# A hybrid trunk layer on one core: more gate tiles as products of x without its norm, a second norm in steps, and no GpSimd arithmetic at the end

## The chip, the core and the metric

The kernel runs on one core of a Trainium2 chip. TensorE (PE) multiplies, VectorE (DVE), ScalarE (ACT) and GpSimd (POOL) work on tiles of 128 partitions, and SyncE, ACT and GpSimd issue DMAs. The time is the device time of one execution in microseconds (us), as the median of several runs. One execution is recorded by the hardware profiler; all rows below are from it.

## What is computed

One layer on 1024 tokens with 1024 features, all in float32:

```python
h = rmsnorm(x, ln1_g)
b_a, c_a, x_a, x_b, g_b, gate_a_logit, gate_b_logit = split(h @ w_in)   # 7 x 1024 columns
y_a = b_a * causal_depthwise_conv(c_a * x_a, conv_a_w)
u_b = causal_depthwise_conv(x_b, conv_b_w, conv_b_b)
y_b = rg_lru(u_b, ...) * gelu(g_b)
merged = (sigmoid(gate_a_logit + bias_a) * (y_a @ w_out_a)
          + sigmoid(gate_b_logit + bias_b) * (y_b @ w_out_b))
x = x + merged @ w_o
h = rmsnorm(x, ln2_g)
x = x + (silu(h @ w_gate) * (h @ w_up)) @ w_down      # 2816 wide
return rmsnorm(x, final_g)

def rmsnorm(x, g):
    return x * rsqrt(mean(x * x) + 1e-6) * g
```

rg_lru is a gated linear recurrence; its decay holds softplus(-lambda).

## The kernel before

**Layout.** Data lie transposed: 128 features on the partitions, 1024 tokens along the row, in two halves H0 and H1 of 512. A tensor of 1024 features is eight such tiles. A matmul takes a 128x128 block of weights and a 128x512 half.

**Precision.** Every operand is split into a high part (ACT, line 114) and the rest (DVE, line 115), and a product is three matmuls (`mm`, line 123): low by high, high by low, high by high. So each tile that PE reads costs ACT and DVE one operation each.

**Products.** Two output tiles of 128 features and the two halves of the tokens form a 2x2 scheme that is worked out with seven products, named P1 to P7, instead of eight (class `Pair`). They need sums of weight blocks (`left_form`, line 240, additions on line 251; the tiles are named s, their splits ws, splits of plain weights wa) and sums of data tiles (`form_steps`, line 149, lines 158 to 175; seven groups, named b11, t1, t2, b21, t3, t4 and b22 in the order they are made). With K = 1024 a product is 12 matmuls, and a pair 84. Results lie in PSUM banks of four tags (a, b, c and x, two banks each) and are combined by `evacuate` (line 282; operations on lines 290 to 318). The products of neighbouring pairs are interleaved: P4 and P3 of a pair come after P5 and P6 of the next.

**Order.** The program emits one product after the other, some of the weight sums of later ones, and after each product at most one step from a queue of background work (`bg`, `tick`). A scheduler puts this into one fixed order for each engine; each engine runs its own list in that order and waits on semaphores. So an operation that waits holds up all behind it on its engine.

**Stages.** (1) The start. x is read, and while the sum of squares of the norm is still running, PE multiplies x without its norm by the weights of four tiles of gate A in ordinary products (line 123 into banks a, b and c for three of them, then into x for the fourth, 48 matmuls): the norm's root R is a factor for each token and can be applied to the result (`std_out`, line 577). R comes from a sum over partitions by matmuls with ones and from `rstd` (line 134: Ln and Exp on ACT, each with a table load, then a Newton step on DVE, lines 141 to 146). Then DVE scales x by R (line 574) and the first forms are made from it. `softplus` (lines 352 to 367) is some 24 small operations for the decay. (2) 26 pairs of the input projection: 20 for the mixers, then gate A (2 pairs) and gate B (4). (3) Mixer stages and the output projections, and the residual x2 with its squares, summed in S2. (4) `norm2` (line 707): root of S2 in two halves, at once, after product P6 of the second pair of the feed-forward stage. 11 times a pair of gate and a pair of up tiles; `ev_fg` (line 717) multiplies by the root, takes Silu and multiplies again (line 715, half tiles), `ev_fu` (line 726) multiplies the two and stores them. (5) The down projection in three groups over its 2304 first rows; the last four tiles of 128 are ordinary products in three pieces of 512, 256 and 256 tokens (`Piece`, line 791), which run with the final norm: each product is added to x2 (line 804), squared on ACT (line 807), the squares of m = 1 to 5 are added on GpSimd (line 809), sums of the rest go through PE (bank x), and `step` (line 825) scales the result: on DVE (line 834), or, for the m in the piece's list `pool`, by ACT (line 813) and GpSimd (line 832).

Of the kernel before, what the change touches and what calls it, by code (L numbers as in the profile page):

```python
# [13 lines left out]
P = 128  # L14
# [13 lines left out]
PIECES = ((0, 512, (1, 4)), (512, 256, (1, 4, 6)), (768, 256, (1, 4, 6)))  # L28
# [21 lines left out]
def trunk(ctx: ExitStack, tc: tile.TileContext, xT, w_first, w_std, w_in, w_ob, w_oa, w_o, w_gu, wd0, wd1, wd2, w_dl,  # L50
# [485 lines left out]

    def first_mm(k):
        for n in range(3):
            std_mm(k, wfs[k], slice(n * P, (n + 1) * P), std[n])
# [3 lines left out]
    R = wide("R")  # L543
    for k in range(KT):
# [11 lines left out]
        if k == 0:  # L556
            nc.scalar.activation(S, x, AF.Square)
        else:
            sq = wide("sq")
            nc.scalar.activation(sq, x, AF.Square)  # L560
            nc.vector.tensor_add(S, S, sq)
        if k == KT - 1:
            sum_split(S, sums, lambda s: wide(s, F32R)[:, :HN])
            for h, b in zip((H0, H1), sums):
                rstd(b, R[:, h], wide("v")[:, :HN], wide("y")[:, :HN])
# [4 lines left out]


    F1 = new_forms()
# [4 lines left out]
    def std_out(c, banks):  # L577
        g = wide("sg")
        for h, b in zip((H0, H1), banks):
            nc.vector.tensor_mul(g[:, h], b, R[:, h])  # L580
        gate_done(c, g, V_GA, dsa)


    last = [bank("x"), bank("x")]
    for i in range(2):
        r = raw_t("raw")
        nc.sync.dma_start(r, w_std[:, 4 * i : 4 * i + 4].rearrange("p k m -> p (k m)"))
        w = split_w(r, "ws")
        for k in range(4 * i, 4 * i + 4):
            std_mm(k, w, slice((k % 4) * P, (k % 4 + 1) * P), last)  # L590
    for c in range(3):
        std_out(c, std[c])
    std_out(3, last)
# [16 lines left out]
    for q in range(2, 4):  # L610
# [95 lines left out]

    def norm2():
        banks = [bank("x"), bank("x")]
        sum_split(S2[0], banks, lambda s: sum_t(s, F32R))
        for h, b in zip((H0, H1), banks):  # L710
            rstd(b, S2[0][:, h], sum_t("v"), sum_t("y"))

    def mul_r(eng, t):
        for h in (H0, H1):
            eng.tensor_mul(t[:, h], t[:, h], S2[0][:, h])

    def ev_fg(i):
        def f(t0, t1):
            for t in (t0, t1):
                mul_r(nc.vector, t)  # L720
# [247 lines left out]
```

## Time and profile before

| | |
|---|---|
| median of three runs | 1548.1 us (1546.53, 1548.1 and 1548.34) |
| profiled execution | 1550.26 us, its span 1548.1 us |
| mean granted clock of PE | 0.978 of full |
| PE busy | 1472.9 us, 95%, 6408 matmul records |
| DVE busy | 1167.0 us, 75% |
| ACT busy | 864.2 us, 56% |
| POOL busy | 149.8 us, 10% |

The span is that of the program on the core; the profiled execution's own time is 2.2 us more. Its time is also 2.2 us above the median. Times inside the span are us from its start. PE's share is that of the whole; at the start, between stages and at the end it is smaller than the mean, and there the timeline of single engines is to be read. The columns of a timeline are start, length, engine, line, operation, tiles (out<-in), shape and count; in brackets stands how long the engine had been idle before, and which operation ended that.

### The profile page before, as it was taken

To read this page: it belongs to the slowest core of one execution; us is meant where nothing else is said; L and a number is where in the kernel's file an instruction comes from. 1 tells how busy PE (TensorE), PEld (TensorE's weight loads), DVE (VectorE), ACT (ScalarE), POOL (GpSimd) and SP (SyncE) were. 2 spreads that over 40 slices of the span, in tenths; PEclk is the share of its full clock that TensorE was granted. 3 is DMA by queue.
4 is the path that set the end of the run, shared out by engine and by line. 5 is a ranking of instruction groups with operands and counts; after the bars stand their busy time and mean duration, and the time that the engine had idled before them with its cause. 6 is when DMAs were issued, how large, how long until landed. Compare 5 with 4: busy or idle time off the path is not lost.

```text
span 1548.1 us, 18200 instructions
## 1 busy us (share of the span) xinstructions
PE 1472.9 (95%) x6408; PEld 1199.2 (77%) x6408; DVE 1167.0 (75%) x1714; ACT 864.2 (56%) x1416; POOL 149.8 (10%) x247
## 2 busy tenths in 40 slices
PE   9889999999999999989999889999999999998995
PEld 7667887878878887868767568888888887776885
DVE  7977758678577459688988986666666679888836
ACT  8559669487596447363456654444444446555532
POOL 1100000001010010201001000000000010112114
PEclk9899999999999999999999989999999999999997
DMA  6211311312213362636344322222222242667603
GB/s 212 75 58 45 116 51 45 123 43 91 81 45 116 114 238 99 231 131 212 111 153 159 104 82 82 82 82 83 83 87 83 82 148 73 243 218 274 199 28 109
DMA packets 75819, 181.61 MB, mean 117 GB/s; under 512 B 8256, under 2 KB 18496, under 8 KB 75728
## 3 DMA queue, kind: packets, MB, share of 16 engines
q1 hardware_dynamic: 48000, 83.71, 17.5%
q0 software_dynamic: 25952, 94.45, 16.7%
q10 hardware_dynamic: 1776, 2.29, 0.4%
q8 instruction: 50, 0.82, 0.2%
q14 instruction: 41, 0.34, 0.1%
HBM read 131.14 MB, written 49.28 MB: 117 GB/s over the span
## 4 chain that ended last, share of the span: by engine, by line
PE 35%; DVE 10%; DMA 3%; issue 3%; ACT 2%; POOL 1%; DVEq 0%; POOLq 0%; ACTq 0%
PE psb L123 15%; PE psc L123 10%; PE psa L123 9%; DMA y<-dmi 2%; DVE t L115 2%; DVE b L115 1%; PE psx L123 1%; DVE ws L115 1%; DMA ld<-dmb 1%; DVE s L251 1%; DMA raw<-in_wd 1%; DVE wa L115 0%; DVE ca L753 0%; DVE ca L318 0%; DVE y L167 0%
## 5 line engine op out<-in xcount | busy, mean ns | idle before, releaser
L123 PE MATMUL psb<-t,ws 128*128 128x512 f32 x1656 | 408.2, 393 | 15.3 <-DVE ws L115 8.7
L123 PE MATMUL psa<-b,wa 128*128 128x512 f32 x1656 | 405.3, 392 | 14.1 <-ACT b L114 11.5
L123 PEld LDWEIGHTS psb<-t,ws 128*128 128x128 f32 x1656 | 311.8, 189 | 87.0 <-DVE ws L115 11.7
L123 PEld LDWEIGHTS psa<-b,wa 128*128 128x128 f32 x1656 | 311.6, 189 | 83.7 <-ACT b L114 13.6
L115 DVE TENSOR_TENSOR ws<-s,ws 128x512 fp32r<-128x512 f32 (+1 forms) x288 | 191.5, 668 | 102.7 <-ACT ws L114 100.8
L114 ACT ACTIVATE ws<-s 128x512 fp32r<-128x512 f32 (+1 forms) x288 | 173.8, 607 | 129.7 <-DVE s L251 63.0
L123 PE MATMUL psc<-t,ws 128*128 128x512 f32 x828 | 209.7, 401 | 15.7 <-DVE ws L115 8.5
L123 PE MATMUL psb<-t,wa 128*128 128x512 f32 x828 | 205.6, 396 | 7.4 <-ACT ws L114 3.8
L123 PE MATMUL psc<-b,ws 128*128 128x512 f32 x828 | 204.7, 390 | 0.0
L123 PEld LDWEIGHTS psc<-t,ws 128*128 128x128 f32 x828 | 159.9, 194 | 54.1 <-DVE ws L115 9.7
L115 DVE TENSOR_TENSOR wa<-raw,wa 128x512 fp32r<-128x512 f32 (+1 forms) x216 | 144.6, 670 | 67.2 <-ACT wa L114 66.5
L123 PEld LDWEIGHTS psb<-t,wa 128*128 128x128 f32 x828 | 157.9, 191 | 43.4 <-ACT ws L114 4.2
L123 PEld LDWEIGHTS psc<-b,ws 128*128 128x128 f32 x828 | 155.6, 188 | 33.3 <-DVE ws L115 0.7
L114 ACT ACTIVATE wa<-raw 128x512 fp32r<-128x512 f32 (+1 forms) x216 | 130.9, 606 | 67.6 <-issue 56.0
L251 DVE TENSOR_TENSOR s<-raw,raw 128x512 f32<-128x512 f32 (+1 forms) x144 | 95.7, 667 | 16.6 <-DMA raw<-in_wd 7.9
L251 DVE TENSOR_TENSOR s<-s,raw 128x512 f32<-128x512 f32 (+1 forms) x144 | 95.7, 665 | 1.8
L290 ACT ACTIVATE psb<-psa 128x512 f32<-128x512 f32 x68 | 39.5, 581 | 73.0 <-PE psa L123 72.9
L318 DVE TENSOR_TENSOR ca<-psc,ca 128x512 f32<-128x512 f32 x72 | 49.6, 689 | 36.5 <-PE psc L123 36.2
L298 ACT ACTIVATE ca<-psb 128x512 f32<-128x512 f32 x68 | 40.3, 593 | 56.6 <-PE psb L123 47.5
L293 ACT ACTIVATE cb<-psc 128x512 f32<-128x512 f32 x68 | 40.3, 593 | 55.8 <-PE psc L123 53.1
L316 ACT ACTIVATE cb<-psb 128x512 f32<-128x512 f32 x58 | 34.4, 594 | 56.3 <-PE psb L123 56.1
L303 ACT ACTIVATE ca<-psa 128x512 f32<-128x512 f32 x62 | 36.6, 590 | 48.5 <-PE psa L123 48.5
(236 smaller groups left out, 1545.4 us busy)
## 6 DMA issues: line engine op xcount, KB each, us to landing
raw<-in_w_in SPq DMA_DIRECT2D x104, 256.0 KB, 3.0
raw<-in_w_gu SPq DMA_DIRECT2D x88, 256.0 KB, 2.9
ld<-dx POOLq DMA_DIRECT2D x24, 512.0 KB, 5.5
y<-dmi POOLq DMA_DIRECT2D x22, 512.0 KB, 7.4
raw<-in_wd SPq DMA_DIRECT2D x48, 192.0 KB, 4.5
dmi<-cb POOLq DMA_DIRECT2D x11, 512.0 KB, 3.1
dmi<-ca POOLq DMA_DIRECT2D x11, 512.0 KB, 2.9
ld<-dsb POOLq DMA_DIRECT2D x8, 512.0 KB, 6.2
```

What stands on the lines that cost most here:

```text
L114: nc.scalar.activation(hi, src, AF.Copy)
L115: nc.vector.tensor_sub(lo, src, hi.bitcast(F32))
L123: nc.tensor.matmul(o, lhsT=l, rhs=r, start=start, stop=stop, skip_group_check=True)
L251: nc.vector.tensor_add(t[:, :c], a[:, :c], b[:, :c])
L290: nc.scalar.activation(b["b"], b["a"], AF.Copy, scale=-1.0)
L293: nc.scalar.activation(t1[:, H1], b["c"], AF.Copy)
L298: nc.scalar.activation(t0[:, H1], b["b"], AF.Copy)
L303: nc.scalar.activation(t0[:, H0], b["a"], AF.Copy)
L316: nc.scalar.activation(t1[:, H0], b["b"], AF.Copy)
L318: nc.vector.tensor_sub(t0[:, H1], b["c"], t0[:, H1])
```

## The change

**Gate tiles.** Six tiles of gate A instead of four are ordinary products of x without its norm: three and one as before, then two more (`w_more`) in the banks c and b. These are 96 more matmuls. The pair of gate A with these two tiles (84 matmuls) is left out of the input stage. Results are scaled, put through the sigmoid and stored by half tiles, in small tiles of the tag `s`, which has five buffers. Tiles 1 and 2 are handled ahead of the scaling of x, tile 0 behind it, and the last three between the groups of forms. The sums of weights for the first products are made between the groups too. The sum of squares is in halves, and softplus comes after the scaling of x.

**Second norm.** `norm2` becomes six steps of the background queue; the operations behind the sum of squares are 1024 wide, with two Ln and one Exp. The steps of `ev_fg` and `ev_fu` go through that queue too.

**The end.** The lists of tiles for GpSimd are gone. DVE adds the squares and makes all outputs. PE sums two squares for the first two pieces and five for the last, instead of three each, and a piece's norm starts one product later.

The rows of PE's order where its 48 matmuls of the fourth gate tile (psx) end and the first products of the input stage begin. psa and psc are banks of tag a and c, b and t are forms of x, wa and ws split weights. Before:

```order
L123 MATMUL psx_465<-h_367,ws_497 128x512
L123 MATMUL psa_717<-b_570,wa_614 128x512 x3
L123 MATMUL psa_717<-b_574,wa_614 128x512 x3
L123 MATMUL psa_717<-b_578,wa_614 128x512 x3
L123 MATMUL psa_717<-b_582,wa_614 128x512 x3
L123 MATMUL psc_739<-t_586,ws_619 128x512
L123 MATMUL psa_806<-b_570,wa_714 128x512 x3
L123 MATMUL psc_739<-t_586,ws_619 128x512 x2
L123 MATMUL psc_739<-t_589,ws_619 128x512 x3
```

After, behind the last of the two new gate tiles (psb):

```order
L123 MATMUL psb_556<-h_384,ws_574 128x512
L123 MATMUL psa_891<-b_715,wa_759 128x512 x3
L123 MATMUL psa_891<-b_719,wa_759 128x512 x3
L123 MATMUL psa_891<-b_723,wa_759 128x512 x3
L123 MATMUL psa_891<-b_727,wa_759 128x512 x3
L123 MATMUL psc_908<-t_731,ws_764 128x512 x3
L123 MATMUL psc_908<-t_734,ws_764 128x512 x3
L123 MATMUL psc_908<-t_737,ws_764 128x512 x3
L123 MATMUL psc_908<-t_740,ws_764 128x512 x3
L123 MATMUL psa_975<-b_715,wa_871 128x512 x3
L123 MATMUL psb_906<-t_768,ws_792 128x512 x3
```

The first three matmuls of the second pair's P1 (psa_806 before, psa_975 after) have moved from within P5 of the first pair to a place between its P5 and its P6 (psb_906).

DVE's order at the second norm. Before, the sum of weights s_7066 with the split ws_7068 stands behind the root (lines 141 to 146, into S_6385):

```order
L146 SCALAR_TENSOR_TENSOR S_6385<-v_7012,y_7013 128x512
L307 TENSOR_TENSOR cb_6977<-cb_6977,psc_6931 128x512
L715 TENSOR_TENSOR ca_6954<-ca_6954,S_6385 128x512
L141 TENSOR_SCALAR v_7020<-psx_6999 128x512
L715 TENSOR_TENSOR cb_6955<-cb_6955,S_6385 128x512
L144 TENSOR_TENSOR v_7020<-v_7020,y_7021 128x512
L145 SCALAR_TENSOR_TENSOR v_7020<-v_7020,y_7021 128x512
L146 SCALAR_TENSOR_TENSOR S_6385<-v_7020,y_7021 128x512
L251 TENSOR_TENSOR s_7066<-raw_6772,raw_6770 128x512
L715 TENSOR_TENSOR ca_6954<-ca_6954,S_6385 128x512
L715 TENSOR_TENSOR cb_6955<-cb_6955,S_6385 128x512
L115 TENSOR_TENSOR ws_7068<-s_7066,ws_7068 128x512
```

After, the same sum and split are s_7080 and ws_7082, and the root's lines are 742 to 747:

```order
L306 TENSOR_TENSOR cb_6989<-psb_6876,cb_6989 128x512
L251 TENSOR_TENSOR s_7080<-raw_6806,raw_6804 128x512
L307 TENSOR_TENSOR cb_6989<-cb_6989,psc_6840 128x512
L742 TENSOR_SCALAR nv_7104<-psx_7060 128x512
L115 TENSOR_TENSOR ws_7082<-s_7080,ws_7082 128x512
L742 TENSOR_SCALAR nv_7104<-psx_7061 128x512
L115 TENSOR_TENSOR wa_7101<-raw_6643,wa_7101 128x512
L312 TENSOR_TENSOR cb_6989<-psb_6876,cb_6989 128x512
L251 TENSOR_TENSOR s_7080<-s_7080,raw_6802 128x512
L746 TENSOR_TENSOR nv_7104<-nv_7104,ny_7085 128x1024
L115 TENSOR_TENSOR ws_7122<-s_7080,ws_7122 128x512
L747 SCALAR_TENSOR_TENSOR nv_7104<-nv_7104,ny_7085 128x1024
```

The sum has moved ahead of the whole root, and the split ahead of all of it but one operation.

DVE's order where the last up pair ends and the forms of the down stage (y, b) are made. Before:

```order
L715 TENSOR_TENSOR ca_9645<-ca_9645,S_6385 128x512 x2
L115 TENSOR_TENSOR ws_9934<-s_9692,ws_9934 128x512
L163 TENSOR_TENSOR y_9753<-y_9753,y_9751 128x512
L115 TENSOR_TENSOR b_9941<-y_9757,b_9941 128x512
L115 TENSOR_TENSOR b_9945<-y_9761,b_9945 128x512
L163 TENSOR_TENSOR y_9757<-y_9757,y_9755 128x512
L163 TENSOR_TENSOR y_9761<-y_9761,y_9759 128x512
L309 TENSOR_TENSOR cb_9793<-psb_9794,cb_9793 128x512
```

After:

```order
L760 TENSOR_TENSOR cb_9649<-cb_9649,S_6419 128x512
L309 TENSOR_TENSOR cb_9797<-psb_9798,cb_9797 128x512
L115 TENSOR_TENSOR wa_9962<-raw_9678,wa_9962 128x384
L175 TENSOR_TENSOR y_9755<-y_9755,y_9757 128x512
L175 TENSOR_TENSOR y_9759<-y_9759,y_9761 128x512
L175 TENSOR_TENSOR y_9763<-y_9763,y_9765 128x512
L115 TENSOR_TENSOR t_9966<-y_9755,t_9966 128x512
L115 TENSOR_TENSOR t_9970<-y_9759,t_9970 128x512
L115 TENSOR_TENSOR t_9974<-y_9763,t_9974 128x512
L764 TENSOR_TENSOR ca_9648<-ca_9648,S_6419 128x1024
```

The second scaling of the gate tiles (line 715 before, line 764 after) has moved behind the evacuation on line 309.

The core of the diff:

```diff
-PIECES = ((0, 512, (1, 4)), (512, 256, (1, 4, 6)), (768, 256, (1, 4, 6)))
+PIECES = ((0, 512), (512, 256), (768, 256))
+    def small(s, dt=F32):
+        return pool["now"].tile([P, HN], dt, tag="s", name=nm(s), bufs=NS)
...
+    def std_out(c, banks):
+        for h, b in zip((H0, H1), banks):
+            g = small("sg")
+            nc.vector.tensor_mul(g, b, R[:, h])
+            nc.scalar.activation(g, g, AF.Sigmoid, bias=col(V_GA, c))
+            nc.gpsimd.dma_start(dsa[c][:, h], g)
...
+    for c in (1, 2):
+        std_out(c, std[c])
+    for k in range(KT):
+        std_mm(k, w4[k // 4], slice((k % 4) * P, (k % 4 + 1) * P), last)
+    more = [[bank(t), bank(t)] for t in "cb"]
+    w5 = [std_w(w_more[i]) for i in range(4)]
+    for k in range(KT):
+        for n in range(2):
+            std_mm(k, w5[k // 2], slice((2 * (k % 2) + n) * P, (2 * (k % 2) + n + 1) * P), more[n])
...
         nc.vector.scalar_tensor_tensor(xs[k], xs[k], col(V_G1, k), R, op0=ALU.mult, op1=ALU.mult)
+    std_out(0, std[0])
     steps = form_steps(xs, F1, range(4))
...
-    for q in range(2, 4):
+    for q in range(3, 4):
         proj(ev_gate(q, V_GA, dsa), c11_act(AF.Sigmoid, V_GA, q))
...
+        bg.extend((parts, sums, root, root2, newton, newton2))
...
+            def silu(t):
+                for h in (H0, H1):
+                    nc.vector.tensor_mul(t[:, h], t[:, h], S2[0][:, h])
                 nc.scalar.activation(t, t, AF.Silu)
-                mul_r(nc.vector, t)
+
+            def scale(t):
+                nc.vector.tensor_mul(t, t, S2[0])
+            bg.extend(lambda g=g, t=t: g(t) for g in (silu, scale) for t in (t0, t1))
...
-            if m in range(1, KT - 2):
-                nc.gpsimd.tensor_add(self.sq[0], self.sq[0], q)
-            else:
-                self.sq.append(q)
-            if m in self.pool:
-                nc.scalar.activation(x, x, AF.Copy, scale=col(V_GF, m))
+            self.sq.append(q)
+            if 2 < m < 6 if o + n == T else m > 1:
+                nc.vector.tensor_add(self.sq[0], self.sq[0], self.sq.pop(1))
...
-            if m in self.pool:
-                nc.gpsimd.tensor_mul(dst, self.xs[m], R)
-            else:
-                nc.vector.scalar_tensor_tensor(dst, self.xs[m], col(V_GF, m), R, op0=ALU.mult, op1=ALU.mult)
+            nc.vector.scalar_tensor_tensor(dst, self.xs[m], col(V_GF, m), R, op0=ALU.mult, op1=ALU.mult)
...
-    for group in steps[2:]:
+    for n, group in enumerate(steps[2:]):
         for g in group:
             g()
+        if n < 3:
+            std_out(3 + n, (last, *more)[n])
+        feed(3 + n)
...
-            if i and m == 1:
+            if i and m == 2:
                 parts[i - 1].norm()
```

## Rows read from the trace of the kernel before

**Rows 1.** The page: PE's share and granted clock, tenths by slice

```profile
PE 1472.9 (95%) x6408; PEld 1199.2 (77%) x6408; DVE 1167.0 (75%) x1714; ACT 864.2 (56%) x1416; POOL 149.8 (10%) x247
...
PEclk9899999999999999999999989999999999999997
```

**Rows 2.** A window: us, busy PE, PEld, DVE, ACT, POOL, granted clock, DMA, GB/s

```profile
920.00:960.00 40.00, 40.00 (x178) 33.10 (x178) 26.60 (x39) 15.97 (x27) 1.07 (x2) 1.00 0.32 98
```

**Rows 3.** Timeline of PE at the start: start, length, work, idle before

```profile
41.57 11.04 PE L123 MATMUL psx<-h,ws 128*128 128x512 f32 x48
...
59.52 0.80 PE L123 MATMUL psa<-b,wa 128*128 128x512 f32 x1 [6.91 <-ACT b L114]
...
89.56 5.46 PE L123 MATMUL psb<-t,wa 128*128 128x512 f32 x12 [3.78 <-ACT ws L114]
...
97.96 2.88 PE L123 MATMUL psc<-b,ws 128*128 128x512 f32 x12
...
103.40 2.88 PE L123 MATMUL psb<-t,ws 128*128 128x512 f32 x12
```

**Rows 4.** Timelines of ACT and DVE at the start

```profile
32.89 0.69 ACT L137 ACTIVATE y<-psx,epst 128x512 f32<-128x512 f32 x1 [0.73 <-PE psx L123]
...
44.40 9.65 DVE L574 SCALAR_TENSOR_TENSOR x<-x,sc,R 128x1024 f32<-128x1024 f32 x8
53.97 0.68 DVE L580 TENSOR_TENSOR sg<-psa,R 128x512 f32<-128x512 f32 x1
...
59.96 1.29 DVE L115 TENSOR_TENSOR b<-x,b 128x512 fp32r<-128x512 f32 x2
...
87.52 0.69 DVE L115 TENSOR_TENSOR wa<-raw,wa 128x512 fp32r<-128x512 f32 x1
```

**Rows 5.** Timeline of POOL, softplus

```profile
38.25 0.49 POOL L361 TENSOR_TENSOR e<-e,e 128x8 f32<-128x8 f32 x1
...
39.46 0.20 POOL L361 TENSOR_TENSOR e<-e,e 128x8 f32<-128x8 f32 x1
```

**Rows 6.** Stores of the four gate tiles (dsa, line 456)

```profile
DMA to landing us min/median/max: 3.0/3.9/6.8
```

**Rows 7.** Timeline of PE at the second norm

```profile
885.98 3.04 PE L123 MATMUL psb<-t,wa 128*128 128x512 f32 x12 [1.00 <-DVE cb L306]
...
905.70 5.49 PE L123 MATMUL psc<-t,ws 128*128 128x512 f32 x12 [7.38 <-DVE ws L115]
...
922.08 2.20 PE L123 MATMUL psb<-t,ws 128*128 128x512 f32 x9
```

**Rows 8.** Timelines of DVE and ACT at the second norm

```profile
884.64 0.68 DVE L251 TENSOR_TENSOR s<-raw,raw 128x512 f32<-128x512 f32 x1
...
892.01 1.28 ACT L138 ACT_TABLE_LOAD   x1
...
893.31 0.63 ACT L138 ACTIVATE y<-y 128x512 f32<-128x512 f32 x1
...
903.14 0.69 DVE L251 TENSOR_TENSOR s<-raw,raw 128x512 f32<-128x512 f32 x1
```

**Rows 9.** Timelines of DVE and PE before the down stage

```profile
1292.08 0.68 DVE L309 TENSOR_TENSOR cb<-psb,cb 128x512 f32<-128x512 f32 x1
...
1292.82 4.61 PE L123 MATMUL psb<-t,wa 128*128 128x512 f32 x12 [1.79 <-DVE cb L309]
```

**Rows 10.** Timelines of PE and DVE at the end

```profile
1519.39 1.56 PE L123 MATMUL psx<-sq,ones_r 128*128 128x256 f32 x6 [0.90 <-POOL sq L809]
...
1532.12 2.48 PE L123 MATMUL psx<-sq,ones_r 128*128 128x256 f32 x6 [2.55 <-POOL sq L809]
...
1535.15 0.42 DVE L141 TENSOR_SCALAR r<-psx 128x256 f32<-128x256 f32 x1 [1.93 <-ACT r L140]
...
1538.65 1.91 DVE L834 SCALAR_TENSOR_TENSOR o<-ca,sc,r 128x256 f32<-128x256 f32 x2
...
1540.48 1.73 DVE L834 SCALAR_TENSOR_TENSOR o<-cb,sc,r 128x256 f32<-128x256 f32 x3
```

More of the change, by code (lines that the diff above doesn't have):

```diff
@@ L569, in trunk, with std_w @@
         first_mm(k)
+    def std_out(c, banks):
[4 more added lines that the diff above has]
+            nc.gpsimd.dma_start(dsa[c][:, h], g)
+    def std_w(src, n=HN):
+        r = raw_t("raw")
+        nc.sync.dma_start(r[:, :n], src)
+        return split_w(r[:, :n], "ws", n)
+    last = [bank("x"), bank("x")]
+    w4 = [std_w(w_std[:, 4 * i : 4 * i + 4].rearrange("p k m -> p (k m)")) for i in range(2)]
+    for c in (1, 2):
[7 more added lines that the diff above has]
+            std_mm(k, w5[k // 2], slice((2 * (k % 2) + n) * P, (2 * (k % 2) + n + 1) * P), more[n])
     F1 = new_forms()
@@ L707, in norm2, with parts, sums, root @@
     def norm2():
[L708 to L715, printed above, removed]
+        S, st = S2[0], {}
+        def parts():
+            st["hi"], st["lo"] = (pool["now"].tile([P, T], F32R, tag="v", name=nm(s), bufs=2) for s in ("nh", "nl"))
+            split(S, st["hi"], st["lo"])
+        def sums():
+            st["b"] = bank("x"), bank("x")
+            for h, b in zip((H0, H1), st["b"]):
+                for i, s in enumerate((st["lo"], st["hi"])):
+                    mm(b, ones_r, s[:, h], i == 0, i == 1)
+        def root():
+            st["y"] = y = late_t("ny")
+            for h, b in zip((H0, H1), st["b"]):
+                nc.scalar.activation(y[:, h], b, AF.Ln, scale=1.0 / D, bias=epst[:, 0:1])
+        def root2():
+            st["v"] = v = late_t("nv")
+            nc.scalar.activation(st["y"], st["y"], AF.Exp, scale=-0.5)
+            for h, b in zip((H0, H1), st["b"]):
+                nc.vector.tensor_scalar(v[:, h], b, 1.0 / D, EPS, op0=ALU.mult, op1=ALU.add)
+        def newton():
+            v, y = st["v"], st["y"]
+            nc.vector.tensor_mul(v, v, y)
+            nc.vector.scalar_tensor_tensor(v, v, -0.5, y, op0=ALU.mult, op1=ALU.mult)
+        def newton2():
+            nc.vector.scalar_tensor_tensor(S, st["v"], 1.5, st["y"], op0=ALU.add, op1=ALU.mult)
+        bg.extend((parts, sums, root, root2, newton, newton2))
     def ev_fg(i):
         def f(t0, t1):
[L719 to L720 removed]
+            gs[i] = t0, t1
+            def silu(t):
+                for h in (H0, H1):
+                    nc.vector.tensor_mul(t[:, h], t[:, h], S2[0][:, h])
                 nc.scalar.activation(t, t, AF.Silu)
[L722 to L723 removed]
+            def scale(t):
+                nc.vector.tensor_mul(t, t, S2[0])
+            bg.extend(lambda g=g, t=t: g(t) for g in (silu, scale) for t in (t0, t1))
         return f
```

51 lines of the change are left out of this document (18 added, 33 removed).

## The prediction, made before the changed kernel ran

> **What bounds the kernel now.** I read the busy times and the slices first: PE is busy for 95% of the span, and its granted clock is full (9 tenths or more) in all slices but a few [rows 1]. So between its gaps the kernel is a chain of matmuls, and a change is worth the PE work that it takes out plus the gaps that it closes. The steady pitch of a 128x512 matmul at full clock comes from the two starts 97.96 and 103.40 with 24 matmuls between them: 5.44/24 = 0.2267 us [rows 3]. The window from 920 to 960 shows the steady state: PE busy all the time, granted clock 1.00, DVE 26.6 of 40 us [rows 2]. Then I went through PE's timeline for gaps. Four places matter. At the start PE waits 6.91 us until 59.52 and 3.78 us until 89.56 [rows 3]; ahead of the first, DVE works without a break: from 44.40 its row of scalings fills 9.65 us, and from 53.97 to 59.96 it goes on at 0.6 for each operation [rows 4]. At the second norm PE waits 7.38 us until 905.70 [rows 7]. Between the up projections and the down stage it waits 1.79 us until 1292.82 [rows 9]. At the end nothing but the last norm is left [rows 10]. Each wait costs twice, since after it the granted clock is at the lower of its levels (1.2 GHz instead of 2.4): of 12 matmuls after 905.70 the row is 5.49 us long, against 2.88 in the steady rows [rows 3, 7].
>
> **The start.** Two more gate tiles become ordinary products, 2 x 48 = 96 matmuls, and one pair with 84 leaves the input stage. By count alone that adds 12 x 0.2267 = 2.7 us; the gain must come from the first gap. PE's 48 matmuls from 41.57 become 144, which last until 41.57 + 144 x 0.2267 = 74.2. The first forms are ready by then, so the wait of 6.91 goes, and P1 of the first pair ends at 76.9. What is late next is DVE. The root's chain on ACT is still two Ln and two Exp with loads of 1.28 between them [rows 8], and two splits now stand in it: from the Ln at 32.89 [rows 4], that is 2 x 0.69 + 2 x 0.63 + 3 x 1.3 + 0.6 = 7.1, until 40.0. Nine half-tile operations on DVE follow, 9 x 0.61 = 5.5, and x is scaled from 45.5 (44.40 before). The eight scalings take 53.97 - 44.40 = 9.6 [rows 4], until 55.1. From there 58 half-tile operations stand ahead of, and with, the split of `wa_871`, on which pair 2's P1 waits; before, (87.52 - 59.96)/45 = 0.612 each [rows 4]. That gives 55.1 + 58 x 0.612 + 0.15 = 90.75. In PE's new order three matmuls of that P1 stand ahead of P6 of the first pair, so PE can't go round them. P5 waits too: its bank holds a gate tile that DVE reads as the 39th of these operations, at 79.0; it runs until 81.7, and then PE idles until 90.8. 108 matmuls later (24.5 us, and 3.0 more for the low clock, as the 24 from 89.56 to 97.96 took 8.4 instead of 5.4 [rows 3]) PE is where it was at 103.40, now at 118.3: 14.9 later. The pair that is gone gives back 84 x 0.2267 = 19.0. **Term: -4.1.** Bounds: if DVE's operations take 0.68, as one alone does [rows 4], the end is 58 x 0.07 = 4 later, and with a longer low clock +1.5 is reached; if the clock costs nothing and two of the gate multiplies fall into waits, about -8.
>
> The softplus chain of some 24 small GpSimd operations now stands beside the forms instead of ahead of them. At 0.2 to 0.5 us each [rows 5] it takes some 8 us on an engine that nobody waits for there, and I cost it at nothing; its user is a pair that comes later. The rule against this is among the rivals. GpSimd's queue gets 12 issues for 4, and takes them after that chain or between.
>
> **The second norm.** Before, PE ended a product at 898.3 and waited until 905.70 for the split of a weight sum [rows 7]. That sum, `s_7066`, could not start on DVE before 903.14 [rows 8], because it is queued behind the root's chain of the second half, and this waits, in each half, for two table loads on ACT like the one at 892.01 [rows 8]. In the changed order the same sum and split (now `s_7080`, `ws_7082`) stand ahead of the first use of the root's input on DVE. What is late instead: the first sum-matmul waits for the 1024-wide low part on DVE, 884.64 + 0.61 for the operation ahead [rows 8] and 1.22 for twice a half: 886.5. PE resumes at 886.6 instead of 885.98 [rows 7]. From 885.98 to 922.08 stand 112 matmuls, which took 36.1 us [rows 7]; without a wait and at full clock they take 112 x 0.2267 = 25.4, so P7 of the pair starts at 912.0. **Term: -10.1.** The evacuations of the two neighbouring pairs, which follow the chain on DVE, come at 896.9 and 899.4 by the same durations, against 898.3 and 901.0, when PE needs their banks. That slack is 1.4 us, so the bound on this side is -6 (a wait of 2 and a low clock of 2); on the other side -11, if the low part is early.
>
> The first Exp starts at 893.31, right as the load that began at 892.01 ends 1.28 later [rows 8]. The Trainium skill, "ScalarE: Activation LUTs", section "What ACT_TABLE_LOAD costs", gives a switch 1283 ns of load and some 1380 ns of drain. The rows show the first and not the second. By the page each of the two remaining loads would be 1.38 later, the second evacuation would come at 902.2 instead of 899.4, PE would wait some 1.2 us and run slowly for a moment, and the term would be about -8.3, the total 1531. I take the row.
>
> **Into the down stage.** P4 of the last pair waits 1.79 for an evacuation on DVE at 1292.08 [rows 9], and the row of its 12 matmuls is 4.61 long instead of 2.88. Counted from the same weight split, this evacuation has 31 operations ahead of it on DVE instead of 35, as four half-tile scalings have moved behind it: 4 x 0.6 = 2.4 earlier. The wait and 1.7 of low clock go, and 0.1 comes back. **Term: -3.4**, between 0 (the scalings turn up ahead after all) and -3.9.
>
> **The end.** PE's last sum waited 2.55 for GpSimd's additions of squares, and the middle piece's sum 0.90 [rows 10]. These additions go to DVE, and so do the scalings that ACT and GpSimd shared. The products, which ended at 1529.5 before (1532.12 less 2.55), end some 2.4 earlier: 0.9 for that wait, 0.4 and 0.7 for one sum-matmul less in each of the two earlier sums, the rest for a slow restart. In the new order the last square addition on DVE stands behind the last product's addition, the end of the middle root (two at 0.4) and three outputs (0.4 each): 1527.1 + 0.4 + 0.8 + 1.1 + 0.3 = 1529.7. The last sum is five matmuls for three; the rows of three are 2.48 long at the low clock and 1.56 at the high one [rows 10]. As PE again idles some 2.5 before it, I take the low: 4.1, so 1533.8. From the old sum's end, 1534.6, to the first output at 1538.65 the root took 4.0 [rows 10], which gives 1537.8. Eight output products on DVE follow at 0.37, the pitch of a 128x256 operation that takes 0.42 alone [rows 10]: 1540.8, against 1540.48 + 1.73 = 1542.2 where GpSimd took a part. **Term: -1.4.** Bounds: +0.5, if each output takes 0.6 as those three did beside GpSimd; -4, if the sum runs at the high clock and the last addition comes right behind the products.
>
> **Sum.** -4.1 - 10.1 - 3.4 - 1.4 = -19.0. The profiled execution took 1550.3, so 1531.3 for one like it; it stood 2.2 above the median of 1548.1, so **1529.1** against that. All upper bounds together give 1544, all lower ones 1521.
>
> **Rivals.** (a) The second norm's wait only moves: the evacuations behind the chain on DVE come after PE needs their banks, and a wait of 2 with 2 of low clock follows. For it speaks the slack of only 1.4; against it that two table loads of four are gone. The term is -6 instead of -10.1: 1533. (b) The start gives nothing, since nine of PE's eleven idle us lie in one stretch, longer than any before, and its low clock may cost more than 3.0; or the scalings before the down stage stay ahead: 1533 if one of them, 1537 if both. (c) GpSimd's chain slows DVE's forms. The rows that are nearest are GpSimd's own, where equal ones take 0.49 and 0.20 [rows 5], while DVE's alone keep to 0.68 [rows 4]. If each of some 24 small operations held DVE up for its length, the forms would be 8 later: start +4, total 1537. The Trainium skill states such a lock on "SBUF — State Buffer", section "SBUF: two separate sides": a DVE operation with two SBUF inputs and a GpSimd operation that reads SBUF block each other for a whole instruction. (d) Slower than before: the five small tiles `s`. A late gate product takes the tile that was stored five tiles before, so DVE, with all forms queued behind it, waits until that store on GpSimd's queue has landed. A landing took 3.0 to 6.8 [rows 6]; the multiply and sigmoid are 0.7 and 0.6, and the closest two uses of one tile on DVE are some 13 us apart. So it costs nothing until a store takes about 11, and 20 us more than that before the whole gain is lost: 1550 and above. The softplus chain ahead of the stores on GpSimd could bring 8 of that, hardly 30.
>
> **How the numbers follow.** Forecast 0.66, reaching from 1523 to 1536 by its own bounds; (a) 0.14; (b) 0.11; (c) 0.04; (d) 0.05, of which 0.03 beyond the old time. The range of 1520 to 1541 holds the forecast, (a), (b), (c) and the near half of (d). A measurement of this kernel can tell about 0.2%, that is 3 us. Faster by more: 0.92, as all of the forecast, (a) and (c) and most of (b) lie under 1545. Within it 0.05: the rest of (b) and part of (d). Slower 0.03.
>
> **What would show it.** Right at the start: PE runs without a gap until some 77, idles for about 11 us in all until 91, and the next long run of matmuls follows a short slow stretch. At the second norm: the row that waits 7.38 at 905.70 is gone, and no wait over 2 us takes its place. Before the down stage: no wait for line 309. At the end: no GpSimd arithmetic, output products of 0.4, and the last sum ending by 1534 less what was gained before it. I am wrong if PE's first gap stays at 7 or over before its first P1, if a new wait of several us stands between 887 and 915, or if DVE in the last pieces, with all outputs and squares on it, makes PE wait for a bank.

## The result, and the profile after

The changed kernel takes 1529.3 us (median of 4 runs, 1528.06 to 1534.14) against 1547.9 for the kernel before (1546.53 to 1548.34). The ratio is 0.9887, with a 95% interval of 0.9864 to 0.991. In a later group of runs it was 1530.3 against 1550.5 (0.9866, 0.9847 to 0.9884). The forecast was 1529.1, in a range of 1520 to 1541. The profiled execution took 1528.26 us, and its span is 1526.5.

The total is right almost to the microsecond. The terms in the two profiled executions are not, and the two errors that matter lie behind the second norm. The table sets the same place of the program in both profiled executions side by side.

| place | before | after | shift | of this stage | predicted |
|---|---|---|---|---|---|
| the product after P2 of pair 2 of the input stage | 103.40 | 117.31 | 13.9, less 19.0 for the pair that is gone | -5.1 | -4.1 |
| P7 of the pair after the second norm | 922.08 | 906.59 | -15.5 | -10.4 | -10.1 |
| P7 of the first down pair | 1303.86 | 1284.66 | -19.2 | -3.7 | -3.4 |
| first of the last ordinary products | 1475.53 | 1458.80 | -16.7 | +2.5 | 0 |
| end of the last output | 1542.21 | 1523.33 | -18.9 | -2.2 | -1.4 |
| end of the span | 1548.1 | 1526.5 | -21.6 | -2.7 | 0 |

The page of the changed kernel, its first part and the line of granted clocks:

```profile
PE 1465.1 (96%) x6420; PEld 1197.1 (78%) x6420; DVE 1166.1 (76%) x1713; ACT 855.2 (56%) x1409; POOL 133.8 (9%) x230
...
PEclk9989999999999999999999999999999999999999
```

PE has 12 records more and is busy 7.8 us less than in [rows 1]: matmuls at the low clock are long, and fewer run there.

**The start.** The timeline of PE in the changed kernel (start, length, work, idle before):

```profile
41.58 11.04 PE L123 MATMUL psx<-h,ws 128*128 128x512 f32 x48
...
74.22 2.88 PE L123 MATMUL psa<-b,wa 128*128 128x512 f32 x12
78.59 3.00 PE L123 MATMUL psc<-t,ws 128*128 128x512 f32 x12 [1.49 <-DVE sg L578]
89.97 1.65 PE L123 MATMUL psa<-b,wa 128*128 128x512 f32 x3 [8.38 <-DVE wa L115]
91.47 4.90 PE L123 MATMUL psb<-t,ws 128*128 128x512 f32 x12
...
98.95 2.88 PE L123 MATMUL psb<-t,ws 128*128 128x512 f32 x12
...
117.31 2.88 PE L123 MATMUL psb<-t,ws 128*128 128x512 f32 x12
```

Set beside [rows 3]: the wait of 6.91 is gone, PE runs on from the gate tiles into the first pair at 74.22 (forecast 74.2), P5 waits for its bank (forecast), and the long wait ends at 89.97 (forecast 90.8), on the split that was named. Both waits together are 9.9 us. The timeline of DVE has what was worked out for it: x is scaled from 45.20 (45.5), the fifth gate tile is read at 77.76, the split comes at 89.23.

```profile
45.20 3.66 DVE L603 SCALAR_TENSOR_TENSOR x<-x,sc,R 128x1024 f32<-128x1024 f32 x3
...
77.76 1.28 DVE L578 TENSOR_TENSOR sg<-psc,R 128x512 f32<-128x512 f32 x2
...
83.78 1.27 DVE L578 TENSOR_TENSOR sg<-psb,R 128x512 f32<-128x512 f32 x2
...
89.23 0.68 DVE L115 TENSOR_TENSOR wa<-raw,wa 128x512 fp32r<-128x512 f32 x1
```

**The second norm.** PE, then ACT:

```profile
881.08 0.47 PE L123 MATMUL psx<-nl,ones_r 128*128 128x512 f32 x1 [1.58 <-issue]
...
892.99 2.88 PE L123 MATMUL psc<-t,ws 128*128 128x512 f32 x12
...
906.59 2.88 PE L123 MATMUL psb<-t,ws 128*128 128x512 f32 x12
```

```profile
881.19 1.28 ACT L736 ACT_TABLE_LOAD   x1
882.48 0.69 ACT L736 ACTIVATE ny<-psx,epst 128x512 f32<-128x512 f32 x1
...
885.16 1.28 ACT L740 ACT_TABLE_LOAD   x1
886.46 1.06 ACT L740 ACTIVATE ny<-ny 128x1024 f32<-128x1024 f32 x1
```

The row that waited 7.38 [rows 7] is now the one at 892.99, without a wait and 2.88 long. PE waits 1.58 once, for the low part of the sum (forecast: 1.6, as 0.6 were added to the old 1.00; this row names no releaser, but with the second norm alone the same wait is 1.62 and names DVE's `nl`). After each table load the Ln and the Exp start 0.01 and 0.02 later. The Trainium skill, "ScalarE: Activation LUTs", section "What ACT_TABLE_LOAD costs", adds a drain of some 1.38 us to a switch; neither trace shows one there, and the smaller term that would follow from it (-8.3) did not come.

**Into the down stage and through it.** PE, then DVE:

```profile
1275.14 2.88 PE L123 MATMUL psb<-t,wa 128*128 128x512 f32 x12
...
1284.66 2.20 PE L123 MATMUL psb<-t,ws 128*128 128x512 f32 x9
...
1291.77 0.50 PE L123 MATMUL psb<-t,ws 128*128 128x512 f32 x1 [0.82 <-ACT psb L290]
1292.52 2.31 PE L123 MATMUL psb<-t,wa 128*128 128x512 f32 x9 [0.25 <-DVE cb L309]
...
1398.37 4.18 PE L123 MATMUL psc<-t,ws 128*128 128x512 f32 x9 [4.93 <-DVE ca L318]
```

```profile
1288.58 1.21 DVE L771 TENSOR_TENSOR ca<-ca,ca 128x1024 f32<-128x1024 f32 x1
...
1290.18 1.21 DVE L771 TENSOR_TENSOR cb<-cb,cb 128x1024 f32<-128x1024 f32 x1
```

P4 of the last up pair has no wait (1275.14; 1292.82 in [rows 9]). One pair later two new waits stand, behind the last products of gate and up on DVE (line 771), which the change has moved there.

**The end.** PE, DVE, and the closing instructions of GpSimd's queue (line 1004, last line of the program: count, then shortest, median and longest in ns, then the first and the last start):

```profile
1513.62 2.43 PE L123 MATMUL psx<-sq,ones_r 128*128 128x256 f32 x10 [3.01 <-DVE sq L853]
```

```profile
1513.14 0.42 DVE L853 TENSOR_TENSOR sq<-sq,sq 128x256 f32<-128x256 f32 x1
...
1522.86 0.47 DVE L871 SCALAR_TENSOR_TENSOR o<-cb,sc,r 128x256 f32<-128x256 f32 x1
```

```profile
L1004 POOLq DRAIN  x3: 40/93/7239, 1458.1 to 1526.2; - x3
```

The same line in the kernel before, and that of SyncE's queue:

```profile
L964 POOLq DRAIN  x3: 40/102/8616, 1538.7 to 1547.9; - x3
L964 SPq DRAIN  x3: 7/7/7, 1545.3 to 1547.6; - x3
```

From the last output on DVE to the end of the span the kernel before needs 5.9 us (1542.21 to 1548.1), the changed one 3.2. The longest of the three drains on GpSimd's queue is the first: before, it began at 1538.7, before GpSimd's last output had run (that ended at 1541.1), and ended 8.6 us later, at 1547.3; the closing semaphores follow (1547.4). SyncE, which waits for the stores, was done at 1545.3, so the drain held the end up by 2.0. In the changed kernel it begins at 1458.1, behind GpSimd's last DMA, and is over long before the end.

### The profile page after: what moved, and what is told of

It reads as the page before. It is cut to its first block, busy times and chain, and to the rows that moved or that the text cites. A ratio compares the mean times of both kernels' runs of the same rounds, so it can differ in the third digit from the quotient of the medians.

```text
span 1526.5 us, 18196 instructions
## 1 busy us (share of the span) xinstructions
PE 1465.1 (96%) x6420; PEld 1197.1 (78%) x6420; DVE 1166.1 (76%) x1713; ACT 855.2 (56%) x1409; POOL 133.8 (9%) x230
## 5 line engine op out<-in xcount | busy, mean ns | idle before, releaser
L123 PE MATMUL psb<-t,ws 128*128 128x512 f32 x1632 | 402.6, 393 | 12.7 <-DVE ws L115 8.7
L123 PE MATMUL psa<-b,wa 128*128 128x512 f32 x1632 | 397.5, 391 | 15.8 <-DVE wa L115 8.4
L123 PEld LDWEIGHTS psb<-t,ws 128*128 128x128 f32 x1632 | 307.9, 189 | 82.9 <-DVE ws L115 11.6
L123 PEld LDWEIGHTS psa<-b,wa 128*128 128x128 f32 x1632 | 306.4, 188 | 82.6 <-DVE wa L115 8.8
L115 DVE TENSOR_TENSOR ws<-s,ws 128x512 fp32r<-128x512 f32 (+1 forms) x284 | 188.3, 666 | 99.3 <-ACT ws L114 97.6
L123 PE MATMUL psc<-t,ws 128*128 128x512 f32 x816 | 204.3, 399 | 11.4 <-DVE ca L318 6.0
L123 PE MATMUL psc<-b,ws 128*128 128x512 f32 x816 | 201.3, 390 | 0.0
L123 PE MATMUL psb<-t,wa 128*128 128x512 f32 x816 | 198.1, 390 | 0.8 <-DVE cb L306 0.5
L123 PEld LDWEIGHTS psc<-t,ws 128*128 128x128 f32 x816 | 156.8, 193 | 48.6 <-ACT b L114 5.3
L123 PEld LDWEIGHTS psb<-t,wa 128*128 128x128 f32 x816 | 152.8, 188 | 34.3 <-DVE cb L309 1.7
```

Of the source, the lines that this page charges most:

```text
L115: nc.vector.tensor_sub(lo, src, hi.bitcast(F32))
L123: nc.tensor.matmul(o, lhsT=l, rhs=r, start=start, stop=stop, skip_group_check=True)
```

## Experiments

Medians are set against the kernel before in the same group of runs: 1549.7 for the first four, 1550.5 for the next four, 1549.6 and 1550.4 for the rest. Single runs of one kernel differ by up to some 9 us (the first experiment's ten lie between 1543.4 and 1551.3), so single traces are compared place by place.

### The three parts, each alone

The theory: the parts are what the table says, and add up. The start alone is the kernel before with the changes from `small` to `std_out`, the order of `softplus`, and one pair less.

```diff
...
-    for q in range(2, 4):
+    for q in range(3, 4):
         proj(ev_gate(q, V_GA, dsa), c11_act(AF.Sigmoid, V_GA, q))
...
```

> The kernel before with the change at the start alone: six ordinary gate tiles, the small half tiles, softplus after the scaling of x, one pair less. If the parts add up, it takes off the 5.1 us by which PE's products of the input stage stood earlier in the changed kernel's trace: some 1542.8 against 1547.9. By the prediction's own term it would be 4.1: 1543.8. If what is gained early is lost again in later waits on transfers, which the changed kernel's down stage could mean, less than 3 is left: over 1545.

Measured: 1546.5, 3.2 less (0.998, 0.9965 to 0.9995). The interval reaches from 0.8 to 5.4 us, so the medians decide between none of the cases. Its trace has the start of the changed kernel again (8.39 us until 89.97), and PE stands 5.3 us earlier than before where the second norm begins (873.14 for 878.48). There its program is the old one, and so is the wait, 7.38 us.

The second norm and the evacuations of gate and up in steps, alone:

```diff
...
+        bg.extend((parts, sums, root, root2, newton, newton2))
...
+            bg.extend(lambda g=g, t=t: g(t) for g in (silu, scale) for t in (t0, t1))
...
```

> The kernel before with the second norm, the gate and the up evacuations in steps, and nothing else. By the trace of the changed kernel the second norm gave 10.4, the way into the down stage 3.7, and the down stage took 2.5 back: 11.6 in all, so some 1536.3 against 1547.9. If the 2.5 had come from the start (products that are earlier and then wait for transfers), the down stage gives nothing back here: 14.1, so 1533.8.

Measured: 1542.3, 7.4 less (0.9948, 0.9932 to 0.9965), short of both. In its trace the way to P7 of the first down pair is 13.0 shorter, at 1290.83, where the two stages gave 14.1 in the changed kernel's. Then 5.4 are lost until the first of the last products. Two rows of PE and one of ACT from this trace:

```profile
1405.91 2.32 PE L123 MATMUL psc<-t,ws 128*128 128x512 f32 x9 [3.42 <-DVE ca L318]
1410.23 3.56 PE L123 MATMUL psb<-t,ws 128*128 128x512 f32 x9 [2.00 <-DVE ws L115]
```

```profile
1389.97 0.63 ACT L114 ACTIVATE b<-y 128x512 fp32r<-128x512 f32 x1 [3.11 <-DMA y<-dmi]
```

ACT, and behind it DVE and PE, wait for tiles y on their way from DRAM: the forms of the next group of the down projection.

The end alone:

```diff
-PIECES = ((0, 512, (1, 4)), (512, 256, (1, 4, 6)), (768, 256, (1, 4, 6)))
+PIECES = ((0, 512), (512, 256), (768, 256))
...
```

> The kernel before with the change at the end alone: squares and outputs on DVE, fewer sums for the first pieces, five for the last, the piece's norm one product later. From the first of the last products to the last output the changed kernel is 2.1 shorter, and from there to the end of the span another 2.7. If the second part belongs to the change (GpSimd has nothing to finish), the gain is 4 to 5: 1543 to 1544. If it was the chance of the one execution, the gain is about 2: 1546. The prediction's term was 1.4.

Measured: 1545.6, 4.1 less (0.9969, 0.9954 to 0.9985). So the closing time belongs to the change; from the last output to the end this kernel takes 3.2. From the first of the last products to the last output its trace gains nothing: 66.8 us, against 66.7 in the kernel before and 64.5 in the changed one.

The three parts alone give 14.6 together, the whole 18.6 and 20.3 in its two groups. Each difference is uncertain by some 2.5 us, and the down stage alone moves by as much from one execution to the next, as the following table shows. Whether a real interaction hides in the missing 4 to 6 us stays open.

### The down stage

From P7 of the first down pair to the first of the last products, in one execution each (the two times stand in the traces as the starts of those products):

| kernel | this stage of the program | us |
|---|---|---|
| before | old | 171.7 |
| start alone | old | 173.0 |
| end alone | old | 175.6 |
| last outputs on DVE (below) | old | 174.1 |
| changed | new | 174.1 |
| changed, second execution | new | 176.8 |
| second norm and evacuations alone | new | 177.0 |

The kernels whose program is the old one here scatter over 3.9 us. So most of the 2.5 of the first table is not shown to be the change's; the profiled execution of before was the shortest of all. Two new waits in this stage are (0.82 and 0.25 at 1291.77): every trace with the evacuations of gate and up in steps and nothing else altered there has them, 0.6 to 1.2 us together, and no trace with these evacuations at once has them. Over all such traces the stage takes 175.5 in the mean of seven with steps and 173.6 in the mean of six without, so the steps may cost some 2 us here. What scatters is PE's idle time (7.7 us of the stage in the kernel before, 9.9 in the one with the end alone) and, by the clock behind the waits, its busy time (164.0 and 165.8). The longest of the waits, for the forms behind the y tiles, lies between 3.1 and 5.1 us in all traces (3.94 in the kernel before, 4.93 in the changed one).

### The steps of gate and up

The changed kernel, with these evacuations at once from the second of the eleven pairs on:

```diff
-            bg.extend(lambda g=g, t=t: g(t) for g in (silu, scale) for t in (t0, t1))
+            if i:
+                for t in (t0, t1):
+                    silu(t)
+                    scale(t)
+            else:
+                bg.extend(lambda g=g, t=t: g(t) for g in (silu, scale) for t in (t0, t1))
...
-            bg.extend(lambda n=n, t=t: step(n, t) for n, t in enumerate((t0, t1)))
+            if i:
+                for n, t in enumerate((t0, t1)):
+                    step(n, t)
+            else:
+                bg.extend(lambda n=n, t=t: step(n, t) for n, t in enumerate((t0, t1)))
```

> The changed kernel itself, beside the others of this group and the kernel before on one chip, as the measure for them: 0.9887 of the kernel before, so some 1530 to 1532 if the kernel before is at 1548 to 1550 here.

> The changed kernel with the gate and up evacuations emitted at once again from the second of the eleven pairs on; the second norm stays in steps. It puts one pair of root scalings of the last gate tiles back ahead of the evacuation on DVE that P4 of the last up pair waits for. If what the trace gave to the way into the down stage (3.7, of which 1.8 are lost again at the next pair) comes from the steps of these evacuations, this kernel loses about 2: 1531.5 for 1529.3, with a wait of about 1 to 2 us at that P4. If the steps matter nowhere but at the second norm, it is the same within 1.

Measured: 1530.3 for the changed kernel itself, 1530.8 (0.9871, 0.9854 to 0.9887) with the edit. They are the same. The row of PE in the edited kernel:

```profile
1275.69 3.01 PE L123 MATMUL psb<-t,wa 128*128 128x512 f32 x12 [0.91 <-DVE cb L309]
```

The wait at P4 is back, without a low clock behind it (3.01), and the two at the next pair are gone. So the steps move some DVE work from the one to the other and gain nothing that can be measured.

The other way round, the last products of gate and up three steps later:

```diff
-            bg.extend(lambda n=n, t=t: step(n, t) for n, t in enumerate((t0, t1)))
+            if i == NFF // 2 - 1:
+                for n, t in enumerate((t0, t1)):
+                    bg.extend([lambda: None] * 3)
+                    bg.append(lambda n=n, t=t: step(n, t))
+            else:
+                bg.extend(lambda n=n, t=t: step(n, t) for n, t in enumerate((t0, t1)))
```

> The changed kernel with the last pair's two multiplications of gate and up (1024 wide, 1.2 us each on DVE) three steps of the background queue later each. They now stand behind the split and the evacuation that PE waits for at the second pair of the down stage (0.82 and 0.25, with a slower pair of rows: some 1.75 in all). Theory: the wait is this work of DVE, moved there by the change; without it 1.5 us less, and none of the two waits there. Rival: DVE is full in that stretch whatever stands first, and the next evacuation is late instead: same within 0.7.

Measured: 1530.8, the same (0.9866, 0.9845 to 0.9887). The two waits are gone, and one pair later there is another:

```profile
1306.29 2.37 PE L123 MATMUL psb<-t,wa 128*128 128x512 f32 x9 [0.85 <-DVE cb L309]
```

DVE's list in this stretch is full; whatever stands first, something is late by about 1 us. And the low clock that followed the 1.79 us in [rows 9] was not the rule either. The kernel with the end alone is the old one at this place, and its row is 3.04 long after a wait of 1.62 (granted clock 1.00 in the 4.65 us from there, 0.64 in the 4.68 us from 1292.82 in the kernel before):

```profile
1291.75 3.04 PE L123 MATMUL psb<-t,wa 128*128 128x512 f32 x12 [1.62 <-DVE cb L309]
```

Last, the second norm in steps on the kernel before, with the evacuations of gate and up at once from the second pair on, as in the first diff of this section:

> The kernel before with the second norm in steps alone; the gate and up evacuations are emitted at once from the second pair on. The trace gave the second norm 10.4 us: 1539.5 against 1550 if nothing is lost behind it. With the evacuations in steps too it was 7.4 less than the kernel before (5.4 us were lost in the down stage of its profiled execution). If it is the down stage's waits for transfers that take this back, whatever the evacuations do, it is again 7 to 8 less: 1542.5. If it was the evacuations in steps, it is over 9 less: under 1541.

Measured: 1540.3, 9.3 less (0.9931, 0.991 to 0.9952). So the norm's own steps carry the gain of that part. The 1.9 between this and the kernel with both is what the evacuations in steps would cost by the expectation and by the means of the down stage, but the two intervals overlap, so it is not shown.

### The first gap

The long wait at the start was forecast as the end of DVE's list. The trace shows one more thing: P6 of the first pair needs a bank of tag b, and DVE reads the sixth gate tile out of these banks only at 83.78, by the order in which the program hands it over. ACT fills that bank at 90.84, behind other operations of its list:

```profile
90.84 0.57 ACT L290 ACTIVATE psb<-psa 128x512 f32<-128x512 f32 x1
```

The edit hands the tile over one group of forms earlier:

```diff
-        if n < 3:
-            std_out(3 + n, (last, *more)[n])
+        if n == 0:
+            std_out(3, last)
+        if n == 1:
+            std_out(4, more[0])
+            std_out(5, more[1])
```

> The changed kernel, with the last gate tile read out of its banks (tag b) right behind the fifth, after the group b21, instead of after t3. Theory: PE's 8.4 us until 89.97 are not the whole work of DVE but one bank: P6 of the first pair needs a bank of tag b, which DVE frees at 85.0 and ACT fills after that, so the first pair's products stand behind three of the second pair, which need the last split of DVE's list. With the bank free at some 81, P6 and P2 run before 88, P7 and the second pair's P1 wait only for their splits, and 36 matmuls stand ahead of where the long wait ended: 7 us less, some 1522. Rival: DVE's list is what it is, and PE waits for it the same 8 us at P7 and after: within 1.5 of 1529.3.

Measured: 1522.2 (0.982, 0.9801 to 0.984), 27.5 less than the kernel before in this group, and by the ratios (0.982 and, in the next group, 0.9866) some 7 less than the changed one. PE in this kernel:

```profile
79.83 3.01 PE L123 MATMUL psc<-t,ws 128*128 128x512 f32 x12 [1.50 <-DVE sg L578]
82.67 2.88 PE L123 MATMUL psb<-t,ws 128*128 128x512 f32 x12
85.39 2.88 PE L123 MATMUL psa<-b,wa 128*128 128x512 f32 x12
88.75 3.06 PE L123 MATMUL psb<-t,ws 128*128 128x512 f32 x12 [0.48 <-DVE ws L115]
...
96.70 4.61 PE L123 MATMUL psc<-t,ws 128*128 128x512 f32 x12 [1.93 <-DVE ws L115]
```

P6 and P2 run while DVE works on; the waits are 3.9 us together instead of 9.9. So most of the gap was one bank that was read late, and not DVE's whole list.

### The squares at the end

PE's last sum waited 3.01 us for an addition on DVE that stands behind the root and three outputs of the piece ahead. The edit puts the additions, and only them, on GpSimd:

```diff
-                nc.vector.tensor_add(self.sq[0], self.sq[0], self.sq.pop(1))
+                nc.gpsimd.tensor_add(self.sq[0], self.sq[0], self.sq.pop(1))
```

> The changed kernel with the additions of squares at the end on GpSimd again (as many as on DVE now), while all outputs stay on DVE. In the changed kernel's trace PE's last sum waits 3.0 us for an addition on DVE that stands behind the middle root and three outputs. If that queue is the price of DVE, the last sum starts some 2 us earlier here and the end comes 1 to 1.5 earlier: 1528. If GpSimd's additions, at 0.72 each beside DVE, are what was slow before, the last sum waits for GpSimd as it did (2.5), and the end is the same or later, 1529 to 1531.

Measured: 1528.5 (0.9854, 0.9837 to 0.9871), 1.8 less than the changed kernel beside it. That is the expected size, though the intervals of the two overlap. The traces are clearer: from the first of the last products to the last output the three with GpSimd's additions (this one and the two of the next section) take 63.3 us each, and the six with DVE's 64.5 to 66.8. The last sum follows the products without a wait:

```profile
1510.07 2.32 PE L123 MATMUL psx<-sq,ones_r 128*128 128x256 f32 x10
```

One output of DVE that met an addition on GpSimd took 1.22 us, and the one behind it 0.74. The rows of the two engines:

```profile
1501.19 1.22 DVE L871 SCALAR_TENSOR_TENSOR o<-cb,sc,r 128x512 f32<-128x512 f32 x1
1502.34 0.74 DVE L871 SCALAR_TENSOR_TENSOR o<-ca,sc,r 128x512 f32<-128x512 f32 x1
```

```profile
1500.65 1.21 POOL L853 TENSOR_TENSOR sq<-sq,sq 128x256 f32<-128x256 f32 x1 [3.58 <-ACT sq L850]
```

The addition, which began while DVE made the output ahead (1500.53 to 1501.27), took 1.21 as well, where others took 0.73 to 0.76 with one at 0.87.

### Both edits together

> The changed kernel with the last two gate tiles read earlier and the squares added on GpSimd, both as measured alone (8 and 1.8 us less than the changed kernel). They lie at the two ends of the program, so they should add up: 1520 to 1521, against some 1550 for the kernel before. If GpSimd beside DVE costs what the earlier last sum gives, 1522.

Measured: 1521.6 (0.9809, 0.978 to 0.9837), the best of all by its ratio, though not apart from the first edit alone (0.982). And with the two gate tiles one group of forms earlier still:

```diff
         if n == 0:
             std_out(3, last)
-        if n == 1:
             std_out(4, more[0])
             std_out(5, more[1])
```

> As the last, with both of these gate tiles read one group of forms earlier still, ahead of the rest of b21. P5 of the first pair then no longer waits 1.5 us for its bank. Theory: DVE's list is now the bound at P7, whose split is the 30th operation behind the first read in either order, so the wait only moves from P5 to P7: same within 0.7. Rival: every wait of PE counts, 1.5 less.

Measured: 1523.9 (0.9821, 0.9796 to 0.9847). No gain: P5 waits no longer, and P7 waits 2.26 instead of 0.50. That far on, DVE's list is the bound. P7 in this kernel:

```profile
87.35 4.61 PE L123 MATMUL psb<-t,ws 128*128 128x512 f32 x12 [2.26 <-DVE ws L115]
```

### The closing drain

> The kernel before with one thing changed: in the last of the three pieces all outputs are made on DVE (GpSimd made three of eight), while GpSimd still adds squares and makes outputs for the first two pieces. Theory: of the end's gain 2.7 us come from GpSimd's closing drain, 8.6 us long from 1538.7 in the kernel before, which ends after the last output has landed. With GpSimd's last work at some 1532 the drain ends by 1540 and the span ends 3.1 after the last output instead of 5.9: 3 us less than the kernel before, with all else alike (the last outputs take 3.2 instead of 3.6). Rival: the 2.7 belong to the squares or the order of the earlier pieces: within 1 of the kernel before.

```diff
-PIECES = ((0, 512, (1, 4)), (512, 256, (1, 4, 6)), (768, 256, (1, 4, 6)))
+PIECES = ((0, 512, (1, 4)), (512, 256, (1, 4, 6)), (768, 256, ()))
```

Measured: 1547.7, 2.7 less (0.9978, 0.9963 to 0.9992). Its last output and the drain:

```profile
1546.06 0.48 DVE L834 SCALAR_TENSOR_TENSOR o<-cb,sc,r 128x256 f32<-128x256 f32 x1
```

```profile
L964 POOLq DRAIN  x3: 40/102/8632, 1535.8 to 1549.4; - x3
L964 SPq DRAIN  x3: 7/7/7, 1548.9 to 1549.2; - x3
```

The drain begins at 1535.8 and ends at 1544.4, ahead of the last output's end at 1546.54, and the span ends 3.2 after that instead of 5.9. SyncE's wait for the stores is the last now, and it is over 2.4 after the last output, where it was 3.1: so of the 2.7, some 2.0 are the drain and 0.7 the last stores, which land sooner. All traces agree: the ten in which the drain is over by the last output end 3.1 to 3.2 us after it, the four with GpSimd's outputs at the very end 5.9 to 6.4. One line of the program carries most of what the change gained at the end.

## Why the prediction was right, and where it was not

- **The start, right.** -4.1 forecast, -5.1 in the trace, 3.2 measured alone with an interval that holds both. The wait ended 0.8 earlier and the low clock cost 2.9 (27 matmuls from 89.97 to 98.95 took 8.98 for 6.12), as forecast. The reason given was too short: the gap was put down to DVE's list, and the experiment shows that some 6 of its 9.9 us hung on one bank.
- **The second norm, right.** -10.1 forecast, -10.4 in the trace, 9.3 measured alone. The wait did not move to the evacuations behind the root: the one at 899.4 by the forecast, as everything there stood 5.5 us earlier, came in time, and PE has no wait between 881.08 and the down stage.
- **Into the down stage, right in the trace and wrong as a reason.** -3.4 and -3.7, but 1.7 of it was a low clock that this one execution showed and others with the same program did not, and the rest stands one pair later as a new wait. The runs show nothing left of this term. The step that failed read a single execution's clock as the price of a wait of 1.8 us, and asked what the moved work leaves ahead of P4, not what it makes late behind it.
- **The down stage, a term that was missing.** It was taken as equal. It differs by 2.5 between the two executions, and by 3.9 among executions with the same program there, in PE's waits and the clock behind them. Of the 2.5, 1.1 are the two new waits, which belong to the change; the rest is not shown to.
- **The end, mis-sized.** -1.4 forecast, -4.1 measured alone. To the last output the term is -2.2 in the trace, but the last sum ran at the high clock in this one execution (2.43), where the five other traces with that sum behind a wait have 3.4 to 4.6, for a forecast 4.1. From the first of the last products to the last output these six traces take 65.9 us in the mean, and the four with the old end 66.5: some 0.5 less is what they show, not 1.4. The clear gain is behind the last output, 2.7. The step that failed took the time from there to the end as equal in both; the profile of before had the row of the drain.
- **The rivals.** (c), GpSimd's small operations beside the forms: the rows below are from the changed kernel. GpSimd's take 0.49 (0.23 to 0.55 over the whole chain), and DVE's four splits 2.50, against 2.52 for four without them in the kernel before. So DVE lost nothing, and GpSimd gave way. The two lengths in [rows 5] show the same: in the kernel before, each of GpSimd's 21 operations of this chain took 0.49 to 0.63 where it began while a DVE operation with two inputs in SBUF was running, as at 38.25 (line 146), and 0.20 to 0.24 where none was, as at 39.46 (line 141 reads PSUM). The Trainium skill, "SBUF — State Buffer", section "SBUF: two separate sides", has either engine block the other; for these short operations the trace shows nothing of it on DVE, and for the longer ones at the end (1.22 and 1.21) it shows it on both. (d), the ring of five small tiles, cost nothing: no read of a gate tile waits for a store.

```profile
61.47 2.50 DVE L115 TENSOR_TENSOR t<-x,t 128x512 fp32r<-128x512 f32 x4
```

```profile
62.33 0.49 POOL L361 TENSOR_TENSOR e<-e,e 128x8 f32<-128x8 f32 x1
...
63.54 0.49 POOL L361 TENSOR_TENSOR e<-e,e 128x8 f32<-128x8 f32 x1
```

DVE in the kernel before:

```profile
38.00 0.68 DVE L146 SCALAR_TENSOR_TENSOR R<-v,y 128x512 f32<-128x512 f32 x1
...
39.21 0.68 DVE L141 TENSOR_SCALAR v<-psx 128x512 f32<-128x512 f32 x1
...
64.78 2.52 DVE L115 TENSOR_TENSOR t<-x,t 128x512 fp32r<-128x512 f32 x4
```

That the total fits to 0.2 us is luck. In the two spans the change is worth 21.6 us, 2.6 more than the forecast 19.0; but the profiled execution of before stood 2.2 above its median and that of after 1.1 below, 3.3 together, so between the medians it is 18.6. The forecast had a term of 3.4 that left nothing and had put at nothing the 2.7 behind the last output.

## What to carry to other kernels

Work that fills a gap (here products that don't need the norm) is worth what the gap was, less what is late next; look then for what frees the banks of the products behind it, since one that was read late cost 7 us. A term that rests on a low clock or on a load's landing in one execution should be checked against a second trace before it goes into a sum. Read the time behind the last output as well: an engine's closing instructions are a stage too.

## What the runs showed of the hardware

- GpSimd closes a program with a drain of 7.0 to 9.1 us in all 14 traces. Its record begins before GpSimd's last arithmetic has ended (1538.7 and 1541.1 in the kernel before). It cost nothing where it began 10.7 us ahead of the end of the last output (in the last experiment); in the kernel before, where it began 3.5 us ahead, it held up the end by 2.0 us.
- After a short wait the granted clock is not always at its lower level: 12 matmuls took 4.61 after 1.79 us of waiting in the kernel before, and at the same place 3.04 after 1.62 and 3.01 after 0.91 in others. After 7.38 and some 8.4 us they were slow in each trace.
- DVE and GpSimd lengthen each other where both read long rows from SBUF (0.74 to 1.22 and 0.73 to 1.21); beside GpSimd's operations on rows of 8 elements DVE kept its times, while those, in the kernel before, took 0.49 to 0.63 where they began beside a running DVE operation with two inputs in SBUF and 0.20 to 0.24 where they did not.
